# A quarter of the attention units transpose their probabilities on TensorE instead of by DMA

## The chip, the cores and the metric

The kernel runs on one core of one Trainium2 chip. The metric is the device time of one execution in microseconds (us), the median of several runs. TensorE (PE in the profile) multiplies matrices into PSUM; VectorE (DVE), ScalarE (ACT) and GpSimd (POOL) work elementwise; SyncE (SP) issues most DMA transfers from a queue of its own. A row "PEld" is the load of a matmul's weights.

## The reference, cut to what matters

The program is one layer of a hybrid decoder: a prompt of 1024 rows and 8 decode rows pass a projection, then attention, a pooling mixer and a gated MLP, then an output projection with a norm. The change touches the two large branches of the prompt's attention, the selected one over all keys and the windowed one over the last 512:

```python
s_s = jnp.einsum('bqkgd,bqksd->bqkgs', qi, g[..., 0, :]) - sl5 * dist_s ...
o_s = jnp.einsum('bqkgs,bqksd->bqkgd', masked_softmax(s_s, mask_s...), g[..., 1, :])
...
s_w = jnp.einsum('bqkgd,bskd->bqkgs', qi, wk[:, :, 0]) - sl5 * dist_w ...
o_w = jnp.einsum('bqkgs,bskd->bqkgd', masked_softmax(s_w, mask_w...), wk[:, :, 1])
```

For each block of 128 queries and each of 8 heads, scores become probabilities P, queries on the partitions. The second product needs P with the keys on the partitions, so every 128x128 block of P has to be transposed. P is float32; it is carried into the matmul as a pair of float16, high part plus remainder.

## The kernel before, in words

The prompt has 8 row blocks of 128 queries, taken in the order `ROWS = (7, 6, 2, 1, 0, 5, 4, 3)`. A row block is cut into units of one head (row blocks 7 to 3), two heads (2 and 1) or four (0): `(i, s0, nh)` is row block i, first head s0, nh heads. There are 50 units. Row block i has nt = i+1 + min(i+1, 5) blocks of 128 keys per head, so a unit of row block 7 has 13 blocks, of 6 12, of 5 11, of 4 10, of 3 8.

The main loop takes one step per unit. In step st it emits:

- `qk` of unit st: score matmuls into PSUM tiles of the pool `sp` (tag s, two tiles of 128x1024 float32 in all), then per branch one DVE instruction (L1344) that adds the position bias and keeps the row maximum, one ACT exponential (L1346) that leaves P in SBUF, and one ACT copy (L1348) to H, P times 1024 in float16;
- `low` of unit st-1: a DVE instruction (L1362) makes the remainder L = 1024 P - H, and SP issues a DMA transpose of L into the second half of the tile T (L1363);
- `high` of unit st: SP issues a DMA transpose of H into the first half of T (L1355);
- some background work that `take` chooses by a budget: projection matmuls (`ps`) in the first row blocks, the output projection (`op`, 24 matmuls of 512 columns for each half of a row block) in the last ones, with the loads and splits of its weights (`wor`, `wo`) between;
- `pv` of unit st-3: three matmuls of 64 columns for each block, with T as weights, into the tile O. After four heads `combine` divides; after eight `finish` gates, writes `yza` and transposes it by DMA to `qa`, from which the output projection of that row block starts.

P, H and L have two buffers each, T three. The output projections of row blocks 4 and 3 take their second half's PSUM tile from `sp` as well. SP and POOL run in the order in which the program was written; the order on PE, ACT and DVE was set by a scheduler when the program was built, and each engine then runs its list in order.

At L817 the decode part already has four float32 128x128 transposes on TensorE, with the same call that the change uses.

Of the kernel before, what the change touches and what calls it, by code (L numbers as in the profile page):

```python
# [10 lines left out]
F32 = mybir.dt.float32  # L11
F16 = mybir.dt.float16
I32 = mybir.dt.int32
AF = mybir.ActivationFunctionType
ALU = mybir.AluOpType
# [12 lines left out]
CE = {}  # L28
# [22 lines left out]
def tile_hymba(ctx: ExitStack, tc: tile.TileContext, A: dict):  # L51
    nc = tc.nc
    V, S, G, Y = nc.vector, nc.scalar, nc.gpsimd, nc.sync
# [3 lines left out]
    sp = ctx.enter_context(tc.tile_pool(name="sp", bufs=2, space=PS))  # L57
# [8 lines left out]
    def mm(out, l, r, st, en):  # L66
        nc.tensor.matmul(out, lhsT=l, rhs=r, start=st, stop=en)  # L67
# [1199 lines left out]
    AT = tc.alloc_tile_pool(name="AT", bufs=1, side="right", reuse_waits="tile")  # L1267
# [13 lines left out]
    def load_qx(i, hf):  # L1281
        t = qx[i, hf] = AT.tile([128, 2, 128], F16, tag="qx", name=f"qx{i}{hf}", bufs=2)
        for k in range(2):
            Y.dma_start(t[64 - k * 64:128 - k * 64], qa[k * 64:k * 64 + 64, i, hf * 4 + k:hf * 4 + 4:2])
# [4 lines left out]
    def spans(i):  # L1289
        n = min(i + 1, 5)  # L1290
        return (0, i + 1, 0), (1, n, i + 1)

    sums = {}

    def qk(u):
        i, s0, nh = u
        nt = i + 1 + min(i + 1, 5)
        P = AT.tile([128, nh, nt * 128], F32, tag="P", name=f"P{i}_{s0}", bufs=2)
        if s0 == 0:
            sums[i] = AT.tile([128, 8, 4], F32, tag="sm", name=f"sm{i}", bufs=2)  # L1300
        sm = sums[i]
        if s0 == 0:
            load_qx(i, 1)
        elif s0 == 4 and i != ROWS[-1]:
            load_qx(ROWS[ROWS.index(i) + 1], 0)
        for h in range(nh):
            s = s0 + h
            k = s % 2
            r = slice(k * 64, k * 64 + 64)
            rx = slice(64 - k * 64, 128 - k * 64)  # L1310
            qy = qx[i, s0 // 4][rx, s % 4 // 2]
            lone = i == 7 and s < PARAM["lone"]
            slope = 2.0 ** -(SLOTS[s][0] * 4 + SLOTS[s][1] + 1)
            ps = None
            banks = []
            cuts = []
            for br, n, o in spans(i):
                T = n * 128
                if ps is None or n > 4 or i > 3:
                    ps = sp.tile([128, 1024], F32, tag="s", name=f"s{i}_{s}_{br}")  # L1320
                    z = 0
                else:
                    z = 512
                lo = (i + 1 - n) * 128
                if i > 3:
                    w = T // 2 if br else max(T // 2, 384)
                    z = 512 - w
                    parts = ((z, lo, w), (512, lo + w, T - w))
                else:
                    parts = ((z, lo, T),)  # L1330
                for a, c0, w in parts:
                    mm(ps[:, a:a + w], qa[:, i, s], ka[br][:, k, c0:c0 + w], True, False)
                    cuts.append((ps, br, a, c0, w))
                banks.append((ps, z))
            for pz, br, a, c0, w in cuts:
                if a == 512 and not lone:
                    mm(pz[:, a:a + w], qy, klx[br][rx, c0 - (384, 0)[br]:c0 - (384, 0)[br] + w], False, True)
                else:
                    mm(pz[:, a:a + w], qa[r, i, s], kl[br][r, c0:c0 + w], False, True)
            for (br, n, o), (ps, z) in zip(spans(i), banks):  # L1340
                T = n * 128
                end = 1024 if br == 0 else 1664
                p = P[:, h, o * 128:o * 128 + T]
                V.tensor_tensor_reduce(p, ps[:, z:z + T], ctt[:, end - T:end], -slope, 3e38, ALU.add, ALU.min,  # L1344
                                       sm[:, s, br:br + 1])
                S.activation(p, p, AF.Exp, bias=sm[:, s, br:br + 1], scale=-1.0, accum_out=sm[:, s, 2 + br:3 + br])  # L1346
        H = AT.tile([128, nh, nt * 128], F16, tag="H", name=f"H{i}_{s0}", bufs=2)
        S.activation(H, P, AF.Copy, scale=1024.0)  # L1348
        return P, H

    def high(u, P, H):
        i, s0, nh = u
        nt = i + 1 + min(i + 1, 5)
        pt = AT.tile([128, 2 * nh * nt, 128], F16, tag="T", name=f"T{i}_{s0}", bufs=3)
        Y.dma_start_transpose(out=pt[:, 0:nh * nt], in_=H.rearrange("p h c -> p (h c)"))  # L1355
        return P, H, pt

    def low(u, P, H, pt):
        i, s0, nh = u
        nt = i + 1 + min(i + 1, 5)  # L1360
        L = AT.tile([128, nh, nt * 128], F16, tag="L", name=f"L{i}_{s0}", bufs=2)
        V.scalar_tensor_tensor(L, P, 1024.0, H, ALU.mult, ALU.subtract)  # L1362
        Y.dma_start_transpose(out=pt[:, nh * nt:2 * nh * nt], in_=L.rearrange("p h c -> p (h c)"))  # L1363
        return pt
# [256 lines left out]
    for i in ROWS:  # L1621
        nh = (4, 2, 2, 1, 1, 1, 1, 1)[i]
# [37 lines left out]
    for st in range(n + 3):  # L1660
        t0 = now[0]
        flush()
        u = units[st - 1] if 1 <= st <= n else None
        if st < n:
            pend[units[st]] = qk(units[st])
        if u is not None:
            pend[u] = low(u, *pend[u])
        if st < n:
            pend[units[st]] = high(units[st], *pend[units[st]])
        bg_step()  # L1670
        if st >= n:
            bg_step()
            take(5.2)
        else:
            i, s0, nh = units[st]
            size = nh * (i + 1 + min(i + 1, 5))
            now[0] += 0.19 * size
            owed = take(owed + (PARAM["s2"] * size if "O" in outp else PARAM["s1"]) - 0.19 * size)
            now[0] = max(now[0], t0 + 0.33 * size + 0.8)
        if st >= 3:  # L1680
            v = units[st - 3]
            pv(v, pend.pop(v))
            e = v[1] + v[2]
            if e % 4 == 0:
                run_post(lambda: combine(v[0], v[1] // 4))
            if e == 8:
                fill.append(outproj(v[0]))
# [171 lines left out]
```

## Time and profile before

| | us |
|---|---|
| median of 3 runs (lowest, highest) | 587.06 (586.46, 589.16) |
| profiled execution | 585.29 |
| its span, first to last instruction | 583.5 |
| PE busy | 519.7 (89%) |
| DVE busy | 441.8 (76%) |
| ACT busy | 323.8 (55%) |
| POOL busy | 197.0 (34%) |
| packets of the DMA queue that SP feeds | 65.2% of 16 engines' span |

The shares are means over stages that have different limits: projection and decode until about 255 us, then the attention of the prompt until 561 us, and a close of 22 us. A busy PE counts overlapping tails of matmuls, so 100% busy means that no wait is left, and not that it is at its peak.

### The profile page before, as it was taken

What the parts mean: (1) busy time and instruction counts of PE and PEld (TensorE: products, weight loads), DVE (VectorE), ACT (ScalarE), POOL (GpSimd) and SP (SyncE); (2) the same over time, 40 slices, a digit from 0 to 9 for tenths busy, and PEclk for the clock granted to TensorE, in tenths of its full rate; (3) what the DMA queues carried; (4) which work ended last, traced back from release to release, by engine and by line L of the source; (5) the groups of instructions that cost most, each with busy time, mean ns of one, the idle gap of its engine ahead of it and who ended that gap; (6) DMA issues with size and microseconds to landing.
All of it is one profiled execution on the core that took longest, in us unless ns stands there. A gap on an engine that the chain in (4) does not pass through costs nothing. (4 is left out here: it accounts for less than half of the span.)

```text
span 583.5 us, 14199 instructions
## 1 busy us (share of the span) xinstructions
PE 519.7 (89%) x5716; PEld 342.7 (59%) x5716; DVE 441.8 (76%) x747; ACT 323.8 (55%) x574; POOL 197.0 (34%) x157
## 2 busy tenths in 40 slices
PE   5889988899999999899999979674599999998974
PEld 3566655589768999666666545442355455454531
DVE  5986489996686667478986987896799788768741
ACT  6444145564553434439656756496487765756600
POOL 1893179403267000045929775132011010000000
PEclk9989999899999999999999998967589999999997
DMA  8613984855675112847898597999969999998952
GB/s 300 260 37 99 253 222 135 244 165 143 206 260 159 39 40 34 239 92 145 171 184 166 97 184 114 125 229 224 124 100 166 182 213 206 177 215 153 199 154 80
DMA packets 199428, 95.31 MB, mean 163 GB/s; under 512 B 168890, under 2 KB 187738, under 8 KB 199362
## 3 DMA queue, kind: packets, MB, share of 16 engines
q1 hardware_dynamic: 195474, 80.85, 65.2%
q0 software_dynamic: 3744, 13.29, 7.3%
q8 instruction: 44, 0.72, 0.5%
q10 hardware_dynamic: 144, 0.26, 0.1%
q14 instruction: 22, 0.18, 0.1%
HBM read 45.43 MB, written 11.86 MB: 98 GB/s over the span
## 5 line engine op out<-in xcount | busy, mean ns | idle before, releaser
L67 PE MATMUL ps<-xh,ws 128*128 128x344 f16 x768 | 175.7, 313 | 5.8 <-DVE t L492 4.3
L67 PEld LDWEIGHTS <-ws 128*128 128x128 f16 x1376 | 129.3, 100 | 87.3 <-issue 17.4
L1346 ACT ACTIVATE P<-P,sm 128x640 f32<-128x640 f32 (+7 forms) x128 | 92.8, 725 | 77.6 <-DVE sm L1344 77.2
L67 PE MATMUL ps<-xl,ws 128*128 128x344 f16 x384 | 120.0, 313 | 0.0
L1362 DVE SCALAR_TENSOR_TENSOR L<-P,H 128x1024 f16<-128x1024 f32 (+4 forms) x50 | 85.0, 1700 | 25.7 <-ACT H L1348 15.3
L1344 DVE CUSTOM_DVE_ANT_0 P<-s,ctt 128x640 f32<-128x640 f32 (+7 forms) x128 | 84.8, 699 | 13.2 <-PE s L67 12.7
L67 PE MATMUL O<-vn,T 128*128 128x64 f16 x1584 | 64.0, 198 | 26.3 <-DMA T<-L 17.1
L67 PEld LDWEIGHTS <-T 128*128 128x128 f16 x1584 | 57.6, 101 | 40.4 <-DMA T<-L 18.9
L67 PEld LDWEIGHTS <-qa 128*128 128x128 f16 (+1 forms) x612 | 44.7, 98 | 61.5 <-issue 33.5
L1348 ACT ACTIVATE H<-P 128x1024 f16<-128x1024 f32 (+4 forms) x50 | 66.3, 1325 | 1.1
L67 PEld LDWEIGHTS <-xh 128*128 128x128 f16 x768 | 60.3, 98 | 0.7
L67 PE MATMUL op<-wo,qa 128*128 128x512 f16 x192 | 46.4, 389 | 3.3 <-DMA qa<-yza 3.3
L67 PE MATMUL s<-ka,qa 128*128 128x384 f16 (+4 forms) x192 | 45.1, 324 | 3.9 <-DVE sm L1344 3.7
L67 PE MATMUL zps<-ws,xh 128*128 128x128 f16 x512 | 45.0, 219 | 0.0
L1534 POOL TENSOR_SCALAR sq<-sq 128x1 f32<-128x1 f32 x8 | 3.9, 492 | 119.4 <-ACT o L1565 119.4
L67 PE MATMUL zps<-ws,xl 128*128 128x128 f16 x256 | 43.6, 219 | 0.0
L67 PEld LDWEIGHTS <-xl 128*128 128x128 f16 x384 | 37.5, 98 | 1.1 <-issue 0.5
L255 ACT ACTIVATE ws<-raw 128x1024 f16<-128x1024 f32 x21 | 22.2, 1056 | 17.6 <-PE ps L67 12.2
L67 PE MATMUL s<-kl,qa 64*128 64x384 f16 (+5 forms) x100 | 30.2, 329 | 0.0
L67 PE MATMUL s<-klx,qx 64*128 64x384 f16 (+4 forms) x92 | 26.9, 323 | 0.0
L1073 POOL TENSOR_TENSOR t<-t,yzc 128x1032 f32<-128x1032 f32 x2 | 4.8, 2382 | 60.4 <-DVE t L492 60.4
L67 PE MATMUL op<-wo,mxg 128*128 128x512 f16 x96 | 24.8, 395 | 0.1
(333 smaller groups left out, 917.5 us busy)
## 6 DMA issues: line engine op xcount, KB each, us to landing
raw<-in_wt_dram SPq DMA_DIRECT2D x21, 512.0 KB, 4.5
wor<-in_wo_dram POOLq DMA_DIRECT2D x8, 512.0 KB, 7.3
xr<-in_xn_dram SPq DMA_DIRECT2D x8, 512.0 KB, 4.8
o_y_dram<-o SPq DMA_DIRECT2D x7, 512.0 KB, 3.9
cr<-in_ccmp_dram SPq DMA_DIRECT2D x24, 128.0 KB, 3.3
o_kww_dram<-in_cwin_dram POOLq DMA_DIRECT2D x8, 259.0 KB, 4.5
o_kww_dram<-in_cwin_dram POOLq DMA_DIRECT2D x8, 252.0 KB, 4.8
xq<-in_xT_dram SPq DMA_DIRECT2D x3, 516.0 KB, 7.6
```

What stands on the lines that cost most here:

```text
L67: nc.tensor.matmul(out, lhsT=l, rhs=r, start=st, stop=en)
L255: S.activation(ws[:, 0, :, a:b], r, AF.Copy, scale=64.0)
L1073: G.tensor_tensor(t, t, hold.pop(f"zc{f2}"), ALU.mult)
L1344: V.tensor_tensor_reduce(p, ps[:, z:z + T], ctt[:, end - T:end], -slope, 3e38, ALU.add, ALU.min, sm[:, s, br:br + 1])
L1346: S.activation(p, p, AF.Exp, bias=sm[:, s, br:br + 1], scale=-1.0, accum_out=sm[:, s, 2 + br:3 + br])
L1348: S.activation(H, P, AF.Copy, scale=1024.0)
L1362: V.scalar_tensor_tensor(L, P, 1024.0, H, ALU.mult, ALU.subtract)
L1534: G.tensor_scalar(sq[:, 2:3], sq[:, 1:2], 1.0 / 1024, sq[:, 0:1], ALU.mult, ALU.add)
```

## The change: what it does

The last unit of each four in row blocks 7 to 3 (heads 3 and 7), and the last unit in row blocks 2, 1 and 0, 13 of 50, take another way to T. They make no H and no L and issue no DMA transpose. In `low`, PE transposes P in float32, eight blocks at a time, into a tile `tp` of the pool `sp`; ACT copies `tp` times 1024 to float16 into the first half of T, and DVE writes 1024 `tp` minus that into the second half. An identity of 128x128 is loaded once.

```diff
--- before.py
+++ after.py
@@ -1291,6 +1291,12 @@
         return (0, i + 1, 0), (1, n, i + 1)
 
     sums = {}
+    ident = AT.tile([128, 128], F32, name="ident")
+    Y.dma_start(ident, A["ce"][:, CE["ident"][0]:CE["ident"][0] + 128])
+
+    def by_pe(u):
+        i, s0, nh = u
+        return (s0 + nh) % 4 == 0 if i > 2 else s0 + nh == 8
 
     def qk(u):
         i, s0, nh = u
@@ -1344,6 +1350,8 @@
                 V.tensor_tensor_reduce(p, ps[:, z:z + T], ctt[:, end - T:end], -slope, 3e38, ALU.add, ALU.min,
                                        sm[:, s, br:br + 1])
                 S.activation(p, p, AF.Exp, bias=sm[:, s, br:br + 1], scale=-1.0, accum_out=sm[:, s, 2 + br:3 + br])
+        if by_pe(u):
+            return P, None
         H = AT.tile([128, nh, nt * 128], F16, tag="H", name=f"H{i}_{s0}", bufs=2)
         S.activation(H, P, AF.Copy, scale=1024.0)
         return P, H
@@ -1352,12 +1360,26 @@
         i, s0, nh = u
         nt = i + 1 + min(i + 1, 5)
         pt = AT.tile([128, 2 * nh * nt, 128], F16, tag="T", name=f"T{i}_{s0}", bufs=3)
+        if by_pe(u):
+            return P, None, pt
         Y.dma_start_transpose(out=pt[:, 0:nh * nt], in_=H.rearrange("p h c -> p (h c)"))
         return P, H, pt
 
     def low(u, P, H, pt):
         i, s0, nh = u
         nt = i + 1 + min(i + 1, 5)
+        if by_pe(u):
+            Pf = P.rearrange("p h c -> p (h c)")
+            for g in range(0, nh * nt, 8):
+                m = min(8, nh * nt - g)
+                tp = sp.tile([128, 1024], F32, tag="s", name=f"tp{i}_{s0}_{g}")
+                for j in range(m):
+                    nc.tensor.transpose(tp[:, j * 128:j * 128 + 128], Pf[:, (g + j) * 128:(g + j) * 128 + 128], ident)
+                t3 = tp.rearrange("p (j q) -> p j q", q=128)[:, 0:m]
+                hi = pt[:, g:g + m]
+                S.activation(hi, t3, AF.Copy, scale=1024.0)
+                V.scalar_tensor_tensor(pt[:, nh * nt + g:nh * nt + g + m], t3, 1024.0, hi, ALU.mult, ALU.subtract)
+            return pt
         L = AT.tile([128, nh, nt * 128], F16, tag="L", name=f"L{i}_{s0}", bufs=2)
         V.scalar_tensor_tensor(L, P, 1024.0, H, ALU.mult, ALU.subtract)
         Y.dma_start_transpose(out=pt[:, nh * nt:2 * nh * nt], in_=L.rearrange("p h c -> p (h c)"))
```

How the instructions then stand, engine by engine. In the names T_3 is the tile T of the unit with first head 3, and so on; the last number only counts allocations.

SP in row block 7, around the unit of head 3. Before:

```order
L1355 DMA_TRANSPOSE T_2_4148<-H_2_4143 128x13x128
L1363 DMA_TRANSPOSE T_2_4148<-L_2_4219 128x13x128
L1355 DMA_TRANSPOSE T_3_4222<-H_3_4217 128x13x128
L243 DMA raw_4232<-in_wt_dram 128x1024
L1284 DMA qx_4311<-qa 64x2x128 x2
L1363 DMA_TRANSPOSE T_3_4222<-L_3_4330 128x13x128
L1355 DMA_TRANSPOSE T_4_4333<-H_4_4328 128x13x128
```

The same place with the change:

```order
L1385 DMA_TRANSPOSE T_2_4148<-L_2_4219 128x13x128
L243 DMA raw_4231<-in_wt_dram 128x1024
L1284 DMA qx_4310<-qa 64x2x128 x2
L1365 DMA_TRANSPOSE T_4_4348<-H_4_4327 128x13x128
L1385 DMA_TRANSPOSE T_4_4348<-L_4_4434 128x13x128
```

Two DMA transposes of 13 blocks are gone, and nothing stands in their place. Over the whole list 26 are gone and one small load (ident) is new; POOL's list is the same.

PE at the same unit, with the change:

```order
L67 MATMUL ps_1_4352<-xh_124,ws_4022 128x344
L67 LDWEIGHTS T_1_4101
...
L67 MATMUL O_0_4268<-vn_92,T_1_4101 128x64
L1377 MATMUL tp_3_0_4329<-ident,P_3_4204 128x128 x8
L1377 MATMUL tp_3_8_4340<-ident,P_3_4204 128x128 x5
L67 LDWEIGHTS T_1_4101
L67 MATMUL O_0_4268<-vn_92,T_1_4101 128x64
```

The 13 transposes stand inside the second product of head 1, and 36 matmuls of that product and 24 of a projection follow before the next score matmul.

PE at the very end. Before, after the last matmul of the last unit's second product (T_7 of row block 3), each first row of a run, and the runs left out between:

```order
L67 MATMUL O_1_8179<-vn_93,T_7_8159 128x64
L67 LDWEIGHTS mxg_4424
L67 MATMUL op_8341<-wo_5973,mxg_4424 128x512
...
L67 LDWEIGHTS mxg_4424
L67 MATMUL op_8370<-wo_5973,mxg_4424 128x512
...
L67 LDWEIGHTS qa
L67 MATMUL op_8341<-wo_6320,qa 128x512
```

With the change:

```order
L67 MATMUL O_1_8297<-vn_93,T_7_8278 128x64
L67 LDWEIGHTS mxg_4439
L67 MATMUL op_8496<-wo_6037,mxg_4439 128x512
...
L67 LDWEIGHTS qa
L67 MATMUL op_8467<-wo_6386,qa 128x512
```

op_8341 and op_8370 are the halves of row block 3's output projection, and op_8467 and op_8496 the same two with the change. Before, 12 matmuls of each half (from mxg and mxp) stood behind the last second product; now those of one half only, and the other half's 12 stand ahead of it.

## Rows read from the trace of the kernel before

**Rows 1.** Busy by stage: PE, PEld, DVE, ACT, POOL, clock, DMA share, GB/s.

```profile
255.00:300.00 45.00, 45.00 (x533) 29.27 (x531) 39.94 (x54) 29.95 (x43) 27.82 (x11) 1.00 0.85 163
300.00:333.00 33.00, 31.37 (x368) 20.55 (x363) 25.71 (x41) 21.27 (x31) 22.75 (x13) 1.00 0.72 136
333.00:437.00 104.00, 75.29 (x859) 46.31 (x857) 84.75 (x196) 70.81 (x159) 34.52 (x30) 0.80 0.92 157
437.00:561.00 124.00, 118.24 (x1234) 62.25 (x1233) 95.34 (x177) 78.58 (x150) 9.17 (x15) 1.00 1.01 190
561.00:584.00 23.00, 12.83 (x70) 5.43 (x69) 7.42 (x11) 2.01 (x5) 0.81 (x2) 0.84 0.27 87
```

**Rows 2.** Whom PE waited for, 333 to 437: total us, times, longest.

```profile
PE O L67 <- DMA T<-L: 13.6, 5, 3.8
PE O L67 <- DMA T<-H: 8.2, 2, 7.8
PE pp L67 <- ACT ocs L1380: 4.4, 1, 4.4
PE s L67 <- DVE sm L1344: 2.2, 5, 0.9
```

**Rows 3.** Whom PE waited for, 437 to 561.

```profile
PE O L67 <- DMA T<-L: 3.5, 4, 2.2
PE oc L67 <- DVE o L1566: 1.4, 1, 1.4
PE O L67 <- DMA T<-H: 0.7, 1, 0.7
```

**Rows 4.** Timeline, 168 to 171: start us, us, engine, line, instruction, count.

```profile
168.90 0.42 PEld L817 LDWEIGHTS s<-cet,stl 128*128 128x128 f32 x4
168.90 0.65 PE L817 MATMUL s<-cet,stl 128*128 128x128 f32 x4
169.39 0.31 PE L67 MATMUL ps<-xh,ws 128*128 128x344 f16 x1
```

**Rows 5.** Groups by form: busy us, mean ns of one.

```profile
L1348 ACT ACTIVATE H<-P 128x1024 f16<-128x1024 f32 x14 | 14.8, 1054 | 0.3
L1348 ACT ACTIVATE H<-P 128x1664 f16<-128x1664 f32 x8 | 12.7, 1583 | 0.1
L576 ACT ACTIVATE thp<-cpsp 128x1024 f32<-128x1024 f32 x2 | 2.0, 1024 | 1.9 <-PE cpsp L67 1.9
L1362 DVE SCALAR_TENSOR_TENSOR L<-P,H 128x1024 f16<-128x1024 f32 x14 | 16.9, 1210 | 8.1 <-DMA T<-L 6.1 <-ACT H L1348 2.0
L577 DVE SCALAR_TENSOR_TENSOR thp<-thp,cpsp 128x1024 f32<-128x1024 f32 x2 | 2.4, 1218 | 2.8 <-ACT thp L576 2.8
```

**Rows 6.** DMA rate in 40 slices of 270 to 300.

```profile
GB/s 217 199 215 201 204 213 208 10 0 154 213 227 88 251 370 168 130 281 219 214 189 229 219 138 22 0 0 62 213 207 216 60 212 287 279 196 71 147 321 258
```

**Rows 7.** Timeline, 386 to 425: SP's and POOL's issues, PE's longest wait.

```profile
394.49 1.44 SPq L1363 DMA_TRANSPOSE T<-L  x1
395.75 1.62 POOL L1467 DMA_DIRECT2D wor<-in_wo_dram  x3
396.04 1.56 SPq L1355 DMA_TRANSPOSE T<-H  x1
397.66 6.46 SPq L1432 DMA_TRANSPOSE qa<-yza  x1
407.43 0.29 PE L67 MATMUL O<-vn,T 128*128 128x64 f16 x2 [7.77 <-DMA T<-H]
```

**Rows 8.** Timeline, 540 to 584: PE.

```profile
541.87 2.76 PE L67 MATMUL op<-wo,qa 128*128 128x512 f16 x12
544.47 0.86 PE L67 MATMUL O<-vn,T 128*128 128x64 f16 x24
560.89 0.81 PE L67 MATMUL O<-vn,T 128*128 128x64 f16 x22 [2.18 <-DMA T<-L]
570.18 6.94 PE L67 MATMUL op<-wo,qa 128*128 128x512 f16 x24 [3.29 <-DMA qa<-yza]
```

**Rows 9.** Busy, clock and DMA, 168 to 170 (columns as in rows 1).

```profile
168.00:170.00 2.00, 2.00 (x34) 1.65 (x32) 1.80 (x7) 0.50 (x2) 1.84 (x1) 1.00 1.00 377
```

## Prediction

> **What bounds the kernel now.** I first cut the attention into stages with the view of busy time by window [rows 1]. From 255 to 333 us (row blocks 7 and most of 6) PE is busy 45.00 of 45 and 31.37 of 33: there PE bounds, and the DMA engines have room (share 0.85 and 0.72). From 333 to 437 (rest of 6, then 2, 1, 0) PE is busy 75.3 of 104, its clock falls to 0.80 of full, and no engine is full, though DVE (84.8) and the DMA engines (0.92) are near it. From 437 to 561 (5, 4, 3) PE is busy 118.2 of 124 at clock 1.00 while the DMA engines are at 1.01: both look full. After that comes a close of 22 us.
>
> Then the view of waits, for PE alone. In the middle stage PE waited 21.8 us for transposed tiles T, 4.4 for ACT and 2.2 for score tiles [rows 2]; in the last stage only 4.2 us for T and 1.4 for something else [rows 3]. So full DMA engines cost PE little there: T comes two units ahead of its use, and PE has other work. Whatever adds to PE in the first and last stages adds to the time; whatever takes from the DMA engines can pay only in the middle, in 21.8 us, and in 4.2 us later.
>
> **The change part by part.** *Added on PE.* The blocks: two units each of 13, 12, 11, 10 and 8, and one each of 12, 8 and 8, in all 136 float32 transposes. The kernel already has four of this very kind: their first start is at 168.90 and the next matmul starts at 169.39, so 0.49/4 = 0.1225 us each [rows 4]. Bounds from the same rows: 0.105 (four loads in 0.42) and 0.1625 (four in 0.65 with the last one's tail). I take 0.1225: 16.7 us in all, between 14.3 and 22.1. By stage: 13+13+12 = 38 blocks or 4.7 us in the first, 12+12+8+8 = 40 or 4.9 in the middle, 22+20+16 = 58 or 7.1 in the last. The 4.9 fall where PE waits anyway, so I cost them at nothing there; if that cover went, they would count.
>
> The Trainium skill, page "TensorE: Matmul & The Clock Gate", part 4 on the PE-mode transpose, gives about 275 ns for a 128x128 bf16 transpose inside a kernel. By that figure the 136 would be an estimated 37 us instead of 16.7. The rows show these transposes overlapping, one finishing each 0.12 us though a single one lasts longer, so the trace disagrees and decides.
>
> *Moved on ACT and DVE.* H becomes a copy out of PSUM, L a subtraction out of PSUM. ACT's copy of 1024 columns is 1.05 us from SBUF and 1.02 from PSUM; DVE's is 1.21 and 1.22 [rows 5]: equal. There are 22 tiles for 13 units, so 9 extra pieces at the fixed part of an instruction. For ACT that is 1054 less 1024 columns at (1583-1054)/640 = 0.83 ns, 0.2 us, so 1.9 us in all, and I take the same for DVE. In the first and last stages PE covers that (DVE 39.9 of 45, 95.3 of 124); in the middle it would count at worst 4 x 0.4 = 1.6 us.
>
> *Removed from the DMA engines and SP.* 26 transposes with 272 blocks of 32.8 KB, 8.9 MB. Slices of transposes alone move 199 to 217 GB/s [rows 6]; at 210 that is 42 us of all engines. By stage: first, PE waits for no T, so nothing is gained. Middle: 80 blocks, 2.6 MB, 12.5 us of DMA time; this is the most that it can pay there. How much of it? The longest wait, 7.77 us, is for H of row block 1's first unit. Its transpose was issued at 396.04, behind L of the unit before (394.49) and together with POOL's loads of output weights (395.75, three of 512 KB), and the next issue on SP stood for 6.46 us [rows 7]. With the change the L at 394.49 is gone, SP is free when H is ready, and H can be ahead of the weights; but then L of the same unit meets them, since POOL's list has not changed. So one part of the 7.77 us comes back and one moves to the next tile. I take half, 4.0 us, with bounds 0 and 12.5. In the last stage I take away all of the 4.2 us of waiting for T.
>
> *Moved on PE at the end.* PE's last wait, 2.18 us, is for L of the last unit, which the change makes itself. But the order shows 12 output matmuls (of mxg and mxp) now ahead of the last second product that stood behind it, where the closing chain hid them. Twelve take 544.47-541.87 = 2.6 us [rows 8]. The chain behind the last product (divide, gate, transpose to qa, 24 matmuls) stays as it is.
>
> *The identity's load* is 64 KB in a stretch before the first transposes; nothing waits for it.
>
> The sum: first stage +4.7; middle -4.0; last +7.1 - 4.2 + 2.6 = +5.5. Together +6.2 us. The profiled execution took 585.29 us (span 583.5), so it would be 591.5; the median of the runs lies 1.8 us above that execution, so 587.06 + 6.2 = **593.3 us**.
>
> **The rivals.**
>
> *The DMA engines bound the middle stage.* Then all 12.5 us come back. For it: share 0.92, and waits for T make up 21.8 of PE's idle time. With the waits the lower clock goes too: PE is busy 75.3 us there at mean clock 0.80, so some 15 us of that is slowness, and I give back a fifth, 3. Against it: DVE is busy 84.8 of 104, and the longest wait falls on a burst that stays. Sum 4.7 - 15.5 + 5.5 = -5.3: 581.8 us. It ends below before as soon as the middle gives more than 10.2.
>
> *The shares balance.* If the middle gives 7.3 to 13.1 us, the sum is within 2.9 us (0.5%, about what a measurement of this kernel can tell from no change): 587.
>
> *The score tiles run short.* `tp` takes its place in the ring of two PSUM tiles that also serves the scores. A tile is held for eight transposes, an ACT copy and a DVE subtraction, 1.0 + 1.05 + 1.22 = 3.3 us, and the next unit's scores wait for both. For it: PE already waits 2.2 us for DVE to free score tiles in the middle [rows 2]. Against it: in the first of these units 36 second-product matmuls and 24 projection matmuls stand between `tp` and the next scores, by the order. If each of the 13 units lost one ACT copy, 1.05 us, it would be 13.7 more: 607 us.
>
> *The clock falls.* The granted clock is 1.00, the 2.4 GHz level, in the window with the four transposes [rows 9], but they are only 0.49 us of it. After a wait of 3.29 us the closing 24 matmuls took 6.94 us, where two times 2.6 is 5.2 [rows 8]: a fall costs 1.7 us. Once in each of 13 units it would be 22 us more: 615 us. The Trainium skill, the same page and part, says that the full clock does not come on for transposes; by that rule this rival would come about, and no run here shows it yet. Against it: the bursts are 0.9 to 1.6 us inside unbroken work, and the matmul that follows the four at 169.39 takes its usual 0.31 us [rows 4].
>
> That the change doesn't do what it says is excluded: SP's list has lost 26 transposes.
>
> **How the numbers follow.** Chances: the forecast (PE's additions outweigh the middle's gain by 3 to 12 us) 0.48; the DMA engines bound the middle 0.20; balance 0.18; short score tiles 0.12; the clock 0.02. Faster by over 0.5% is 0.20, within 0.5% 0.18, slower 0.62. The lower end takes the full 12.5 of the middle and the cheapest transpose (4.0 - 12.5 + 6.1 - 4.2 + 2.6 = -4.0): 583. The upper end adds to the forecast a good half of the score tiles' price: 602. That leaves out most of the clock's case, the dearest part of the score tiles' and the deepest of the DMA's, no more than 2 in 10. The forecast's own range is 590 to 599.
>
> **What would show it right or wrong.** Right: 136 rows of `tp` on PE, spaced by about 0.12 us; the first stage longer by 4 to 6 us with PE as full as before; waits for T in the middle down from 21.8 by a few us, with one long wait still beside POOL's weight loads; in the last stage the DMA share clearly under 1 and PE still full; the last second product not waiting. Wrong, towards faster: the middle shorter than 104 us by 10 or more and its clock near 1; or PE's rows of `tp` cheaper than 0.1 us. Wrong, towards slower: PE waiting for DVE or ACT at score tiles near each `tp`, or DVE waiting for `tp`; a clock under 1 in the first or last stage.

## The result, and the profile after

The changed kernel takes 611.94 us (median of four runs, 604.81 to 612.49), the kernel before 588.11 beside it: 1.0415 of before, 95% interval 1.0358 to 1.0471. Slower was forecast, but 593.3 us, and 611.94 lies above the upper end of 602. The profiled execution took 611.68 us, with this head of its page:

```profile
span 609.0 us, 14457 instructions
PE 541.7 (89%) x5852; PEld 360.7 (59%) x5852; DVE 440.9 (72%) x756; ACT 324.5 (53%) x583; POOL 189.8 (31%) x157
```

To find the stage, I cut both traces at the same places of the work: the first softmax pass on VectorE of row block 7, of row block 2 and of row block 5, the last pass of all, and the end. This is busy time by window for the kernel before (columns as in [rows 1]: window, its length, PE, PEld, DVE, ACT, POOL, clock, DMA share, GB/s):

```profile
251.70:357.10 105.40, 98.88 (x1144) 64.45 (x1143) 87.71 (x131) 68.57 (x100) 71.20 (x39) 0.98 0.79 148
357.10:433.10 76.00, 52.18 (x526) 30.78 (x525) 62.09 (x159) 52.18 (x128) 17.18 (x16) 0.75 0.94 157
433.10:551.00 117.90, 114.32 (x1255) 60.89 (x1255) 94.34 (x174) 78.03 (x147) 8.37 (x13) 1.00 1.01 188
551.00:583.50 32.50, 20.65 (x149) 9.78 (x147) 12.21 (x22) 5.85 (x14) 1.61 (x4) 0.90 0.47 120
```

and for the changed kernel:

```profile
254.40:360.60 106.20, 103.90 (x1157) 67.96 (x1155) 85.34 (x135) 67.57 (x101) 66.42 (x38) 0.98 0.65 123
360.60:435.50 74.90, 52.90 (x600) 34.89 (x601) 58.64 (x157) 51.66 (x127) 14.31 (x16) 0.79 0.66 133
435.50:574.50 139.00, 127.55 (x1287) 68.78 (x1284) 99.15 (x185) 79.47 (x156) 8.08 (x13) 0.96 0.64 129
574.50:609.00 34.50, 22.07 (x171) 11.01 (x169) 12.37 (x22) 6.72 (x15) 1.62 (x4) 0.85 0.44 110
```

The span grew by 25.5 us: 2.7 ahead of the attention (where the profiled executions of the experiments below take 251.6 to 259.4 us for the same work, so this is within their scatter), +0.8 in row blocks 7 and 6, -1.1 in 2, 1 and 0, **+21.1 in 5, 4 and 3**, +2.0 in the close. In those three row blocks the DMA share fell from 1.01 to 0.64, as forecast, and yet PE is less full: idle 139.00 - 127.55 = 11.45 us instead of 3.58. The other 13.2 us are busy time: 58 transposes (row block 0's last eight among them, row block 3's last eight come later) and matmuls at the lower clock level (mean 0.96 instead of 1.00). By estimate that is 7.1 us at the forecast's 0.1225 each, and 0.04 of 127.55, some 5 us.

The waits of PE there (total us, times, longest) answer to [rows 3]. Before, 433.1 to 551:

```profile
PE oc L67 <- DVE o L1566: 1.4, 1, 1.4
PE O L67 <- DMA T<-L: 1.4, 3, 0.8
PE O L67 <- DMA T<-H: 0.7, 1, 0.7
```

and in the changed kernel, 435.5 to 574.5:

```profile
PE O L67 <- DMA T<-H: 6.3, 5, 2.3
PE s L67 <- DVE sm L1350: 2.4, 2, 1.3
PE O L67 <- DMA T<-L: 2.1, 4, 0.8
PE O L67 <- ACT T L1380: 0.4, 1, 0.4
```

PE waits for the tiles that still go by DMA, 8.4 us where it was 2.1, and hardly for the ones it transposes itself (0.4). The turn from row block 4 to row block 3 shows why. Timeline of the changed kernel, 533 to 600 (start, us, engine, line, instruction, count, [idle before]):

```profile
533.95 0.39 PE L67 MATMUL s<-kl,qa 64*128 64x512 f16 x1
...
536.61 0.71 PE L1377 MATMUL tp<-ident,P 128*128 128x128 f32 x5
...
538.30 1.28 SPq L1365 DMA_TRANSPOSE T<-H  x1
...
538.75 1.29 ACT L1380 ACTIVATE T<-tp 128x1024 f16<-128x1024 f32 x2
...
539.80 1.28 DVE L1561 SCALAR_TENSOR_TENSOR o<-o,sq,xr 128x1024 f32<-128x1024 f32 x1 [3.45 <-DMA xr<-in_xn_dram]
...
541.00 1.22 DVE L1384 SCALAR_TENSOR_TENSOR L<-P,H 128x1024 f16<-128x1024 f32 x1
...
542.39 0.28 PE L67 MATMUL O<-vn,T 128*128 128x64 f16 x2 [2.34 <-DMA T<-H]
...
542.80 1.54 DVE L1381 SCALAR_TENSOR_TENSOR T<-tp,T 128x1024 f16<-128x1024 f32 x2
542.88 2.72 PE L67 MATMUL op<-wo,mxg 128*128 128x512 f16 x6 [0.20 <-DVE sq L1590]
...
550.89 0.59 PE L67 MATMUL s<-ka,qa 128*128 128x512 f16 x2
551.09 0.60 ACT L1587 ACTIVATE o<-op 128x512 f32<-128x512 f32 x1 [11.06 <-PE op L67]
...
556.35 1.24 SPq L1365 DMA_TRANSPOSE T<-H  x1
...
559.50 1.46 PE L67 MATMUL op<-wo,mxg 128*128 128x512 f16 x6
...
594.53 7.97 PE L67 MATMUL op<-wo,qa 128*128 128x512 f16 x24 [5.93 <-DMA qa<-yza]
```

Read it from 536.61: the ten transposes of row block 4's last unit take both score tiles. ScalarE copies them at 538.75, but VectorE's subtractions stand in its queue behind a row block's output (which waits 3.45 us for its input row) and behind the other unit's L; they start at 542.80 and end at 544.34. From the first transpose to the end of the last read that is a hold of 7.7 us. It is the longest of the 13 units; worked out from the timelines in the same way, all 13 come to 75 us, 5.8 each, and a full tile of eight blocks is held for 5.1 us on average.

PE meanwhile waits 2.34 us for a T whose H went out at 538.30. Then it goes through the 24 output matmuls that stand next in its fixed list, at first at the lower clock level: the granted clock is 0.50, the 1.2 GHz level, from 544 to 548, after 2.8 us in which PE was busy for 0.34:

```profile
540.00:542.80 2.80, 0.34 (x4) 0.18 (x3) 2.80 (x4) 0.04 (x1) 0.00 (x0) 0.83 1.20 225
544.00:548.00 4.00, 4.00 (x11) 1.37 (x10) 0.35 (x2) 0.00 (x0) 0.00 (x0) 0.50 0.21 38
```

Six of these matmuls take 2.72 us, where six take 1.46 at 559.50. The next scores start at 550.89, 16.5 us after the last, ScalarE sits idle for 11 us, and the next H goes out at 556.35, 18 us after the one at 538.30.

One thing is easily misread here. PE has no wait in front of the scores at 550.89: both tiles had been free for 6.5 us, and in the whole stage PE waits only 2.4 us for score tiles. The scores are late because the list has the 24 output matmuls ahead of them. Before the change no stretch without a score matmul is over 5.8 us in these row blocks; now six are over 6 us. Why the scheduler laid the list out so is not on record. That the shared ring is behind it is an inference, on which the experiments with another ring bear.

### The profile page after: what moved, and what is told of

Same layout as the page of the kernel before. It is cut to its first block, busy times and chain, and to the rows that moved or that the text cites. A ratio compares the mean times of both kernels' runs of the same rounds, so it can differ in the third digit from the quotient of the medians.

```text
span 609.0 us, 14457 instructions
## 1 busy us (share of the span) xinstructions
PE 541.7 (89%) x5852; PEld 360.7 (59%) x5852; DVE 440.9 (72%) x756; ACT 324.5 (53%) x583; POOL 189.8 (31%) x157
## 4 chain that ended last, share of the span: by engine, by line
PE 38%; DVE 18%; DMA 15%; issue 11%; ACT 8%; SPq 7%; POOL 2%; DVEq 0%; POOLq 0%; ACTq 0%
PE ps L67 12%; PE op L67 6%; PE zps L67 5%; PE s L67 4%; DVE P L1350 4%; DMA T<-L 3%; ACT P L1352 3%; PE O L67 3%; DMA xr<-in_xn_dram 3%; SPq L296 3%; DVE L L1384 3%; PE v1ps L67 2%; ACT H L1356 2%; PE tp L1377 1%; DMA o_ps_dram<-dsh 1%
## 5 line engine op out<-in xcount | busy, mean ns | idle before, releaser
L67 PEld LDWEIGHTS <-ws 128*128 128x128 f16 x1376 | 128.5, 99 | 85.3 <-issue 16.5
L67 PE MATMUL O<-vn,T 128*128 128x64 f16 x1584 | 66.9, 197 | 31.0 <-DMA T<-H 17.8
L67 PEld LDWEIGHTS <-qa 128*128 128x128 f16 (+1 forms) x612 | 46.8, 100 | 70.0 <-issue 39.7
L1384 DVE SCALAR_TENSOR_TENSOR L<-P,H 128x1024 f16<-128x1024 f32 (+4 forms) x37 | 63.4, 1717 | 17.9 <-ACT H L1356 17.9
L67 PE MATMUL op<-wo,qa 128*128 128x512 f16 x192 | 49.7, 407 | 5.9 <-DMA qa<-yza 5.9
L1356 ACT ACTIVATE H<-P 128x1024 f16<-128x1024 f32 (+4 forms) x37 | 49.2, 1329 | 0.7
L67 PE MATMUL s<-kl,qa 64*128 64x384 f16 (+5 forms) x100 | 31.6, 331 | 0.0
L1588 DVE TENSOR_TENSOR o<-op,gpb 128x512 f32<-128x512 f32 x16 | 11.0, 689 | 26.4 <-ACT o L1587 26.4
L67 PE MATMUL s<-klx,qx 64*128 64x384 f16 (+4 forms) x92 | 29.0, 325 | 0.0
L1381 DVE SCALAR_TENSOR_TENSOR T<-tp,T 128x1024 f16<-128x1024 f32 (+4 forms) x22 | 21.0, 975 | 8.5 <-ACT T L1380 8.5
```

Of the source, the lines that this page charges most:

```text
L1381: V.scalar_tensor_tensor(pt[:, nh * nt + g:nh * nt + g + m], t3, 1024.0, hi, ALU.mult, ALU.subtract)
L1588: V.tensor_tensor(o32[:, c], ps, outp["gpb"][:, c], ALU.mult)
```

## The experiments

Every ratio is to the kernel before on the same chip, with its 95% interval.

### Where: the change in some row blocks only

```diff
-        return (s0 + nh) % 4 == 0 if i > 2 else s0 + nh == 8
+        return i > 5 and ((s0 + nh) % 4 == 0 if i > 2 else s0 + nh == 8)
```

and in the same place `i < 3` and `2 < i < 6` for the other two.

**Row blocks 7 and 6.** 

> The change in row blocks 7 and 6 alone (4 units, 50 of the 136 transposes), where TensorE hardly waits. If TensorE's own work is the price (50 transposes at 0.12 to 0.15 us), the kernel is 6 to 7.5 us slower than before. If the price is score tiles that a late VectorE holds, which the trace shows in the last stage, it is 5 us slower at most, about what the shift was at the first unit of row block 2 (+1 us). If any new static order of the engines costs time, whatever is edited, some 10 us.

**Row blocks 2, 1, 0.** 

> The change in row blocks 2, 1 and 0 alone (3 units, 28 transposes), where the DMA queues were over 90% busy before. If the transfers bounded this stage, 4 us faster than before, as forecast for the stage. If the stage is bounded by the chain of one unit (scores, P, H and L, transfer, second product), no gain: within 2 us of before. The trace after shows waits on T of 22.2 us there against 21.8 before, which speaks for the second.

**Row blocks 5, 4, 3.** 

> The change in row blocks 5, 4 and 3 alone (6 units, 58 transposes), where the trace after loses most, some 20 us. If TensorE's own work is the price, 7 to 9 us slower than before (less the 4.2 us of waits for T that go). If score tiles held by a VectorE that is late with its subtractions are the price, 13 to 20 us slower, with a stretch in which no score matmul starts for over 8 us after the transposes of a unit.

Measured 1.0122 (1.0073 to 1.0170), 1.0013 (0.9977 to 1.0050) and 1.0193 (1.0141 to 1.0246): 7.2, 0.8 and 11.3 us. They add up to 19.3, near the 24 of the whole. The first would be 0.143 us for each of 50 transposes, within the forecast's bounds, but its interval (4.3 to 10.0 us) takes in all three of its expectations, and its trace does not put the time into row blocks 7 and 6, which are 0.8 us longer, as in the change:

```profile
256.30:362.50 106.20, 103.93 (x1157) 67.91 (x1155) 85.41 (x136) 67.58 (x101) 66.37 (x38) 0.98 0.64 123
```

Behind its transposes it too has stretches of 8.4 to 10.0 us without a score matmul; the third kernel has four of 9.6 to 11.1. The third's 11.3 us lie between its two expectations and decide for neither. The second is the forecast's middle stage by itself, and nothing is won. Its windows (cut as above) show where the time went:

```profile
363.00:432.10 69.10, 50.98 (x562) 31.85 (x563) 58.40 (x155) 48.95 (x124) 16.57 (x16) 0.85 0.80 154
432.10:554.70 122.60, 113.89 (x1218) 60.52 (x1215) 96.96 (x180) 79.83 (x152) 9.11 (x13) 0.99 0.89 173
```

The middle is 6.9 us shorter, and the next stage, in which only the tail of one transposed unit lies, 4.7 us longer and the close 1.6: PE's idle time fell from 23.8 to 18.1 us in the middle and rose from 3.6 to 8.7 in the last row blocks. It moved.

### What: transfers removed, transposes, and who reads the score tiles

In the first of these kernels T is filled from P in SBUF and nothing is transposed; in the second the transposes are made into score tiles that nobody reads.

```diff
-                tp = sp.tile([128, 1024], F32, tag="s", name=f"tp{i}_{s0}_{g}")
-                for j in range(m):
-                    nc.tensor.transpose(tp[:, j * 128:j * 128 + 128], Pf[:, (g + j) * 128:(g + j) * 128 + 128], ident)
-                t3 = tp.rearrange("p (j q) -> p j q", q=128)[:, 0:m]
+                t3 = Pf.rearrange("p (j q) -> p j q", q=128)[:, g:g + m]
```

**No transposes.** 

> As the change, all 13 units, but without the transposes: T is filled by ScalarE and VectorE straight from P in SBUF, so that the output is not the reference's. It keeps the 26 transfers removed, the copies and the subtractions, and leaves out the 136 transposes and the score tiles that they take. If the price of the change is TensorE's own work or the score tiles, it is faster than before by 4 to 10 us (the waits for T that go). If it is the new static order or the work of VectorE and ScalarE, it stays 5 us or more slower than before.

**Transposes, unread.** 

> As e4_notr, with the 136 transposes put back into score tiles that nobody reads, so a score tile is free again as soon as TensorE is done with it (T is still filled from P, so the output is not the reference's). e4_notr measured 0.990 of before. If TensorE's own work is the whole price of the transposes, this comes to the time of the change, 1.04 of before. If it is only 136 times 0.12 to 0.15 us, 16 to 20 us over e4_notr, 1.017 to 1.024, and the rest up to the change is what the reading holds up.

Measured 0.9898 (0.9853 to 0.9943) and 0.9997 (0.9965 to 1.0030). Removing 26 transfers is worth 6 us if no transposes replace them. The 136 transposes by themselves cost 1.0% or 5.8 us, less than the 16 expected. The two traces show a balance of both signs. Row blocks 2, 1 and 0, then 5, 4 and 3, without them:

```profile
361.50:434.80 73.30, 51.60 (x578) 31.43 (x578) 60.88 (x160) 50.80 (x128) 14.78 (x15) 0.77 0.71 132
434.80:550.10 115.30, 113.63 (x1179) 60.06 (x1177) 95.54 (x181) 79.09 (x153) 9.29 (x13) 0.96 0.82 159
```

and with them:

```profile
355.40:425.00 69.60, 51.52 (x614) 33.92 (x611) 61.19 (x167) 53.23 (x132) 14.59 (x17) 0.88 0.76 144
425.00:547.20 122.20, 118.50 (x1235) 66.04 (x1235) 95.18 (x177) 78.48 (x150) 10.80 (x13) 0.97 0.76 154
```

In the last three row blocks, where PE is nearly full, the traces are 6.9 us apart for 58 transposes, 0.12 each, as forecast (single executions scatter by some 2 us there). In the middle as many busy microseconds hold 36 matmuls more, and the stage is 3.7 us shorter, at clock 0.88 instead of 0.77. That the transposes raised the clock is not shown: kernels without any in the middle have 0.75 to 0.82 there, kernels with the change's transposes there 0.77 to 0.88. Unread, the kernel takes as long as before, so the change's 24 us over before come in only when the transposed tile is read.

**Score tiles held, few transposes.** Of each tile only the first transpose is made; both engines read it for every block.

```diff
-                for j in range(m):
+                for j in range(1):
...
-                t3 = tp.rearrange("p (j q) -> p j q", q=128)[:, 0:m]
+                t3 = tp.rearrange("p (j q) -> p j q", q=128)[:, 0:1].to_broadcast([128, m, 128])
```

> As the change, but of the transposes of each score tile only the first is made, 22 in all for 136; ScalarE and VectorE read it once for each block, so copies, subtractions and the hold of the 22 score tiles stay, and most of TensorE's work goes (the output is not the reference's). If score tiles held by late subtractions cost the 10 us that TensorE's work doesn't explain, 22 times 0.15 and 10 us over e4_notr: 1.007 to 1.015 of before. If the hold costs nothing, 0.99 to 1.0.

Measured 1.0070 (1.0038 to 1.0102): 10 us over the kernel without transposes, with 22 of them for 136. The hold costs, with little of TensorE's work. Beside the change it says more: every reader is in place here, and the 114 transposes left out are worth 20 us, though 136 unread cost 5.8. Over the kernel without transposes, the transposes alone come to 5.8 us and the hold with few of them to 10, but both together, in the change, to 30. No run separates where the other 14 come from.

**One column read late.** Behind each subtraction from P in the unread kernel:

```diff
+                V.tensor_copy(one1, tp[:, 0:1])
```

> As e5_unread (all 136 transposes into score tiles, T filled from P, output not the reference's), but VectorE copies one column of each transposed tile behind the subtraction, 22 copies of one column, so that the score tile is held as long as in the change. e5_unread measured 1.000 of before, the change 1.04. If the hold of the score tiles by a late VectorE is the price, this comes to 1.025 to 1.04. If ScalarE's and VectorE's reading of float32 from PSUM, or T coming later, is the price, it stays at 1.00 to 1.01.

Measured 1.0110 (1.0073 to 1.0146): a late read of one column by VectorE costs 6.6 us over the unread kernel, a miss for the expectation that this hold would be all of the price.

**Either reader alone.** In one kernel only ScalarE's copy, in the other only VectorE's subtraction reads `tp`; `p3` is the same piece of P in SBUF.

```diff
-                V.scalar_tensor_tensor(pt[:, nh * nt + g:nh * nt + g + m], t3, 1024.0, hi, ALU.mult, ALU.subtract)
+                V.scalar_tensor_tensor(pt[:, nh * nt + g:nh * nt + g + m], p3, 1024.0, hi, ALU.mult, ALU.subtract)
```

```diff
-                S.activation(hi, t3, AF.Copy, scale=1024.0)
+                S.activation(hi, p3, AF.Copy, scale=1024.0)
```

**ScalarE reads.** 

> As the change, but VectorE subtracts from P in SBUF and only ScalarE reads the transposed score tile (the output is not the reference's): the tile is held up to ScalarE's copy alone, and T still waits for the transposes. If VectorE's late reading is what makes the change dear, 1.00 to 1.015 of before. If it is that T comes only behind the transposes, 1.03 to 1.04.

**VectorE reads.** 

> The other half: ScalarE copies from P in SBUF, and VectorE reads the transposed score tile in its subtraction (the output is not the reference's). If VectorE's late reading is the price, 1.025 to 1.04 of before, well above e13_hi; if ScalarE's waiting behind the transposes is, 1.00 to 1.015.

Measured 1.0236 (1.0181 to 1.0291) and 1.0173 (1.0117 to 1.0229). Over the unread kernel (0.9997) that is 14 and 10 us, together the 24 of both. The two intervals overlap, so neither reader is shown to be the dearer one, and neither theory as I had put it holds: VectorE's lateness is not the whole. The totals add up, but the places differ. The last three row blocks, with ScalarE reading alone and with VectorE alone:

```profile
441.30:563.30 122.00, 117.56 (x1217) 65.21 (x1216) 96.17 (x179) 79.41 (x152) 7.87 (x13) 0.97 0.71 147
435.80:562.10 126.30, 122.67 (x1288) 67.85 (x1285) 98.12 (x183) 79.85 (x154) 7.86 (x13) 1.00 0.69 142
```

Unread it is 122.2 us, in the change 139.0. So by these traces a single reader costs 4 us at most there and the two, one behind the other, 17. ScalarE's 14 us lie in other stages.

### Which ring

**Another ring for the transposed pieces**, that of the output projections, so that no score tile is taken:

```diff
-            for g in range(0, nh * nt, 8):
-                m = min(8, nh * nt - g)
-                tp = sp.tile([128, 1024], F32, tag="s", name=f"tp{i}_{s0}_{g}")
+            for g in range(0, nh * nt, 4):
+                m = min(4, nh * nt - g)
+                tp = fp.tile([128, 512], F32, tag="f", name=f"tp{i}_{s0}_{g}")
```

> As the change, with each transposed piece in a 512-column tile of the ring of two in which the output projections accumulate, so that no score tile is taken; twice as many, half as large copies and subtractions for the 13 units. If the hold of score tiles costs 8 to 10 us, 1.022 to 1.03 of before, as far as the projections' tiles are not the next to run short. If not, 1.04 or more, since the number of instructions rises.

**That ring in row blocks 5, 4, 3 only.** 

> As the change, with the projections' ring of 512 columns for the transposed pieces in row blocks 5, 4 and 3 alone, and score tiles in the other seven units. e7_fring, with that ring everywhere, measured 1.011, the change 1.04. If the score tiles are dear in the last three row blocks, where the trace of the change loses 21 us, 1.01 to 1.02. If they are as dear everywhere, 1.025.

**That ring in 7, 6, 2, 1, 0 only.** 

> The complement: the projections' ring in row blocks 7, 6, 2, 1 and 0, score tiles in row blocks 5, 4 and 3. If the last three row blocks hold the price, 1.03 to 1.04 of before, near the change; if the score tiles are as dear everywhere, 1.025.

Measured 1.0111 (1.0071 to 1.0151), 1.0149 (1.0098 to 1.0199) and 1.0278 (1.0212 to 1.0343). All 136 transposes, both readers and T behind the transposes are still there, with 15 pieces more; 18 of the 24 us are gone. PE's waits in the last three row blocks of the first of these kernels, 429.9 to 556.4:

```profile
PE tp L1377 <- DVE T L1381: 1.5, 2, 1.0
PE O L67 <- DMA T<-H: 1.0, 2, 0.6
PE O L67 <- DMA T<-L: 0.9, 1, 0.9
```

It now waits for VectorE at `tp` itself, and the waits for T are down from 8.4 to 1.9 us. With the other ring in the last three row blocks alone 16 us are back, with it in the rest alone 8. The window of the last three in the second and in the third of these kernels:

```profile
436.00:561.10 125.10, 119.38 (x1270) 67.39 (x1267) 98.96 (x192) 80.55 (x161) 9.47 (x13) 0.97 0.75 146
```

```profile
431.60:569.50 137.90, 132.08 (x1328) 72.70 (x1329) 99.23 (x183) 79.80 (x155) 10.29 (x14) 0.96 0.63 130
```

125.1 without transposed pieces in score tiles there, 137.9 with them, beside 139.0 in the change. The pieces are half as large as well, and the list of every engine is a new one. Small pieces in the scores' ring, which would tell ring from size, were not run.

**The same without row blocks 7 and 6** (`i < 6 and` in the rule above). 

> As e7_fring (1.011 of before), but not in row blocks 7 and 6, where e1_rows76 found 1.012 for the transposes alone. If the parts add up as e1 to e3 did, 7 us less than e7_fring: 0.997 to 1.002 of before. If the other stages' gain was only the luck of one order, up to 1.01.

Measured 1.0130 (1.0078 to 1.0182): a miss. 50 transposes less save nothing here, though in the kernel with score tiles in row blocks 7 and 6 alone they cost 7 us.

### Other mends

**Tile free after ScalarE.** ScalarE copies in float32 over P, GpSimd and VectorE work from there.

```diff
-                S.activation(hi, t3, AF.Copy, scale=1024.0)
+                S.activation(w, t3, AF.Copy, scale=1024.0)
+                G.tensor_copy(hi, w)
```

> As the change, but ScalarE copies the transposed tile in float32 over P, GpSimd makes the high half from there and VectorE the low half: the score tile waits for ScalarE alone, at the price of 22 copies on GpSimd, which is nearly idle in the last stage. If VectorE's late subtractions held the score tiles, 1.02 to 1.03 of before. If the hold is not the price, 1.04 or above, since T comes later.

**Written ahead of the next scores.** For these units `low` is called before `qk` of the next.

```diff
+        if u is not None and by_pe(u):
+            pend[u] = low(u, *pend[u])
         if st < n:
             pend[units[st]] = qk(units[st])
-        if u is not None:
+        if u is not None and not by_pe(u):
```

> As the change, with the transposes, the copy and the subtraction of these units written ahead of the next unit's scores instead of behind them, so that VectorE's subtraction doesn't queue behind the next unit's softmax passes. If the hold is the price and it ends sooner, 1.015 to 1.03 of before. If the order of writing has no effect on the hold or the hold is not the price, 1.035 to 1.045.

**That order with the other ring, without 7 and 6.** 

> e10_fring_no76 and e11_lowfirst in one: the projections' ring, not in row blocks 7 and 6, written ahead of the next scores. If the hold was the price, it is gone already in e10, so the same as e10_fring_no76 within 0.5 percent. If the order of writing is worth something by itself, 0.99 to 0.995 of before.

Measured 1.0292 (1.0251 to 1.0332), 1.0578 (1.0527 to 1.0629) and 1.0181 (1.0129 to 1.0233). Freeing the tile after ScalarE brings back 7 us, as expected if VectorE's late reads held it. The second is a miss, outside both its ranges: writing it ahead makes things worse by 9.6 us with score tiles and by 3 without (there the intervals overlap). By the program the transposed pieces then stand in front of the scores from which the next H comes; that this is the cause was not traced.

### How much is the order alone

**Other units of the four.**

```diff
-        return (s0 + nh) % 4 == 0 if i > 2 else s0 + nh == 8
+        return s0 % 4 == 0 if i > 2 else s0 == 4
```

> The change with other units: in row blocks 7, 6, 5, 4 and 3 the first unit of each four is transposed on TensorE instead of the last, in row blocks 2 and 1 the same half of the second four, in row block 0 the same unit; as many transposes, copies and score tiles, in another static order. If the price lies in the score tiles and in T behind the transposes, 1.03 to 1.045 of before. If the change met a bad order by chance, 1.01 to 1.02.

**The kernel before with another number.** In its table of parameters, `"s2": 0.52` becomes `0.5`.

> The kernel before, with 0.50 instead of 0.52 us of output projection released for each block of a unit, nothing else: some 10 projection matmuls stand elsewhere in the last row blocks, in another static order of all engines there. It shows what a new order costs by itself. If the order alone costs as much as the change, 1.02 or more of before; if not, 1.00 within 0.01.

Measured 1.0320 (1.0267 to 1.0373) and 1.0013 (0.9971 to 1.0055). One other order is worth nothing, but it is a small step: set side by side, PE's lists of the two kernels differ in some 350 of 5716 instructions, with the change in some 1,660. The same work at other places is slower by 3.2% instead of 4.2%, with intervals that just overlap. So most of the price stays in another order, and some 5 us may be this order's own. Differences of that size between two of the kernels above may be their orders' too.

## Why the prediction was wrong, by its steps

The step that failed is the last stage: +5.5 us were forecast for it, and the last three row blocks and the close took 23.1 more. Two of its terms were wrong, the -4.2 for the waits and the nothing for the reads out of PSUM.

- **136 transposes at 0.1225 us:** right in size. The first unit's 13 in the changed kernel start within 1.3 us, 0.11 us apart, and unread they cost 0.12 each where PE is nearly full:

```profile
L1377 PE MATMUL tp<-ident,P x13: 272/273/306, 281.3 to 282.6; 128*128 128x128 f32 x13
```

- **First stage, +4.7:** PE's busy time rose by 5.0 us, the length by 0.8 only, since PE's idle time there fell from 6.5 to 2.3 us. Over the whole of these row blocks PE was not as full as in the windows of [rows 1].
- **Middle, -4.0:** -1.1, which is not clear of the scatter of single executions: three kernels that leave these row blocks as they were have 72.8, 73.9 and 77.2 us there, where it was 76.0. PE's wait for T from 360.6 to 435.5 is 10.7 + 9.3 = 20.0 us, where it was 10.7 + 8.2 = 18.9 before, cut at the same places (21.8 in the longer window of [rows 2]), with the DMA share down from 0.94 to 0.66. So lighter DMA engines did not shorten the waits. Where the middle did get shorter, as in the kernel with the change there alone, the time came back later.
- **Last stage, -4.2 of waits for T: this step failed.** I took away all of them, though 18 of the 24 units of that stage still go by DMA. Cut at the same places of the work they were 2.1 us and became 8.4, and PE's idle time grew by 7.9. The DMA share fell to 0.64 and did not help: a transfer goes out when its H is made, and H came late behind scores that stand late in PE's list. Behind such waits the clock fell to its lower level.
- **Reads out of PSUM, covered by PE: this step failed too.** The sum counts the length of the copies and subtractions, not how long they keep a score tile. Unread, the transposes leave the kernel as long as before, so the 24 us come with the reads; with another ring and smaller pieces 18 of them go. (A slip without effect: two of the nine extra pieces lie in the middle, not four, so that bound would be 0.8 us and not 1.6.)
- **+2.6 of output matmuls moved ahead of the last product:** right. PE's last wait is 5.93 us instead of 3.29 [rows 8], 2.64 more.
- **The rival of short score tiles** had the place right and the price too low. I counted 3.3 us of hold, each operation following the last at once, and one copy lost in each unit, 13.7 us. In the trace a full tile is held for 5.1 us on average and 7.4 at most, since the readers stand in queues, and the loss comes by way of the list: its sign, PE waiting at score tiles, shows only 2.4 us in the last stage. I had given it 0.12.
- **The rival of the falling clock** fell, in the form that the transposes themselves bring it down. Through the first unit's 13 transposes the granted clock is 1.00, the 2.4 GHz level:

```profile
281.25:282.85 1.60, 1.60 (x22) 1.59 (x21) 0.70 (x2) 1.60 (x2) 1.52 (x2) 1.00 0.81 264
```

The Trainium skill, "TensorE: Matmul & The Clock Gate", part 4, says that the full clock doesn't come on for them. Here it had come on with the matmuls around them and stayed; no run has transposes alone, so none tests that sentence. The clock did fall, behind waits, as at 542.88, for some 5 us in the last stage by the estimate above, against the rival's 22. That its 615 us are near the measured 611.94 is chance.

The Trainium skill, "PSUM — Partial Sum Buffer", summary of rules for kernel authors, asks to empty PSUM promptly. The runs point the same way: moving the 22 tiles out of the scores' ring, in smaller pieces, brought 18 us back.

Open stays how the shared ring becomes a later place of the scores in PE's list, and whether the ring or the size of the pieces counts for more. Open stays also what ScalarE's reading alone pays for with 14 us. Worked out as above, its holds sum to 42 us over 13 units, 57 where VectorE reads alone, 75 in the change; the kernel with the shortest holds is not shown to be the faster of the first two, so the sum of holds doesn't look like the measure.

## What to carry to other kernels

Before giving a buffer of a full ring a second user, ask who reads it last and what stands ahead of that reader in its queue, and then what the ring's first user feeds: here two score tiles feed every H that a transfer waits for. A price worked out from operation times alone is a lower bound for a hold: 3.3 us counted, 5.1 measured on average. Where an engine runs a fixed list, look for the loss in the list and not only in the waits. And a transfer that is waited for need not be a transfer that is slow: follow its source back to the queue that made it before you expect a gain from less traffic.

## What I had not expected of the hardware

Back to back among other matmuls, float32 transposes on TensorE start 0.11 us apart, though each lasts 0.27 us, and the granted clock stays at 1.00 through 13 of them. 136 that nobody reads cost 5.8 us altogether, a balance of 0.12 each in the last three row blocks and a shorter middle. Who reads them out of PSUM, and when, cost four times as much here.
